# List of surplus blocks of a mixture-of-experts layer: with a slot per partition, by small products, in three steps

## The chip, the cores and the metric

The kernel runs on one core of a Trainium2 chip. The metric is the device time of one execution in microseconds (us); the time before is the median of three runs. The engines are TensorE (PE, with its weight loads shown apart as PEld), VectorE (DVE), ScalarE (ACT), GpSimd (POOL) and SyncE (SP), which issues the weight loads to the DMA engines.

## What is computed

One decoder layer on 1024 tokens of width 1024: a token mixer (a projection, two convolutional branches, gates, an output projection), a mixture of experts with 32 experts of which each token takes two, an embedding gate, and a final norm. What the change touches is the expert part. The reference sorts the 2048 assignments by expert, pads each expert's rows to blocks of 128 and runs every block:

```python
flat_e = expert_id.reshape(n_assign)              # 2048 assignments
counts = jnp.bincount(flat_e, length=N_EXPERTS)   # rows of each of 32 experts
padded = (counts + ROW_BLOCK - 1) // ROW_BLOCK * ROW_BLOCK
...
def expert_block(args):
    xb, e = args
    a = xb @ w_gate[e]
    b = xb @ w_up[e]
    return (jax.nn.silu(a) * b) @ w_down[e]
```

## The kernel before

The token mixer fills the first 830 us; w_o and the router follow, then the experts (950 to 1490 us), then the embedding gate and the final norm. All arithmetic is in fp32 or in products of split fp32 parts.

**Slots.** The 32 experts are put into 32 slots by rank of their row count. Each slot has a kind, a letter in SLOTS, that fixes how many rows it computes: L 32 rows, N 64, M 128, S 96, X 160, B 256 (two blocks of 128), A 352 in three units. Which expert sits in a slot is known on the chip only (slots, srow). Blocks of 128 rows are "wide" (class Wide): each weight tile is split into two parts on ACT and DVE (split, L99 and L100), in 24 parts a unit through a ring of four, and each part gives three products a block (L869). Narrower blocks (class Rows) multiply the unsplit weights (L928 gate and up, L955 down).

**The loop.** For unit u in order of slots: the activation of u (L932), the first three quarters of the first half of gate and up of u+1, the transposes of u's hidden rows into bank h and their copy (L941, L942), the last of that half, **a step of the list if the slot is in SIZES (18, 19, 21, 22)**, p_step (from slot 18 on it transposes p through banks x0 and x1, L110, and copies them out on DVE, L1164; later it multiplies them, L1173), the down product of u (L955), the copies of its result into ys (L966, half on ACT, half on DVE), and the transposes of unit u+2's gathered rows into x0 (and x1 for some), copied to its activation tile xt (L819 and L821; for wide blocks L828 and the splits). PE, ACT, DVE and SP issue in the order in which the program is written; POOL's order is a scheduler's.

**The list.** A slot may get more rows than its kind has. The surplus goes in blocks of 128 through a loop behind the last slot, guarded by the number of blocks. Its list (ovi: 30 experts, 30 first rows, one count) is worked out on DVE in one partition, in four steps: sizes0 (blocks of each slot by eight compares, a running sum by five shifts and adds), sizes1 and sizes2 (compares of 30 entries by 32 slots, 960 elements, and their sums), sizes3 (scaling and casts). The steps sizes1 and sizes2 take a scratch tile from the ring of three that holds the activation tiles: xtile(), mp.tile([128, 2048], dt, name="xt", bufs=3).

**Weights.** Six loads of 1 MB a slot, issued by SP (L678) into a pool of 1 MB buffers (about three slots' worth); a buffer comes free when the products of its slot are done, or for wide slots when its last part is split.

Of the kernel before, what the change touches and what calls it, by code (L numbers as in the profile page):

```python
# [10 lines left out]
F32 = mybir.dt.float32  # L11
# [5 lines left out]
OP = mybir.AluOpType  # L17
AX = mybir.AxisListType
# [5 lines left out]
NT = 8  # L24
KT = 8
KB = 31
NE = 32
DE = 512
CAP = 1024
# [3 lines left out]
NOV = 30  # L33
# [7 lines left out]
PARTS = 4  # L41

RETIRE = 42
SIZES = (18, 19, 21, 22)


A0, A1, A2, B1, B2, B3 = range(6)
# [20 lines left out]
def layer_kernel(ctx: ExitStack, tc: tile.TileContext, A, out, dbg=None):  # L68
    nc = tc.nc
    w_in = A["w_in"][0]  # L70
    dram = ctx.enter_context(tc.tile_pool(name="dram", bufs=1, space=DRAM))
    const = ctx.enter_context(tc.tile_pool(name="const", bufs=1))
# [11 lines left out]
    def tpsum():  # L84
        return psum.tile([128, 512], F32, name="tp", bufs=2)
# [27 lines left out]
    ident = const.tile([128, 128], F32, name="ident")  # L113
# [17 lines left out]
    place = const.tile([NE, NE], F32, name="place")  # L131
    cap_row = const.tile([1, NE], F32, name="cap_row")
    srow = const.tile([1, 2, NE], F32, name="srow")
    iota_s = const.tile([1, NE], F32, name="iota_s")
    ovi = const.tile([1, 2 * NOV + 1], I32, name="ovi")


# [38 lines left out]
    with tc.tile_pool(name="s0", bufs=1, side="right") as s0:  # L176
# [39 lines left out]
        with tc.manual_schedule(engines={mybir.EngineType.Pool, mybir.EngineType.DVE, mybir.EngineType.Activation}):  # L216
# [3 lines left out]
            tp = tpsum()  # L220
# [12 lines left out]
        tp = tpsum()  # L233
# [7 lines left out]
    with tc.tile_pool(name="s1", bufs=2) as s1:  # L241
        for cb in range(8):
# [18 lines left out]
            for t in (1, 2):  # L261
                nc.vector.scalar_tensor_tensor(c3, m[:, t:t + T], cw[:, cb, KB + t:KB + t + 1], c3,
                                               op0=OP.mult, op1=OP.add)
# [3 lines left out]
            for t in range(1, KB):  # L267
                nc.vector.scalar_tensor_tensor(acc, u[:, t:t + T], cw[:, cb, t:t + 1], acc,  # L268
                                               op0=OP.mult, op1=OP.add)
# [3 lines left out]
    rt = mix.enter_context(tc.tile_pool(name="rt", bufs=1, side="right"))  # L273
# [14 lines left out]
            nc.gpsimd.iota(pay[:, :, k, j], pattern=[[128, NT]], base=T * k * j, channel_multiplier=1)  # L288
    iota_e = rt.tile([128, NE], F32, name="iota_e")
    nc.gpsimd.iota(iota_e, pattern=[[1, NE]], base=0, channel_multiplier=0, allow_small_or_imprecise_dtypes=True)  # L290
    nc.gpsimd.tensor_copy(iota_s, iota_e[0:1])
    iota_r = rt.tile([128, 64], F32, name="iota_r")
    nc.gpsimd.iota(iota_r, pattern=[[1, 64]], base=0, channel_multiplier=0, allow_small_or_imprecise_dtypes=True)

# [25 lines left out]
        nc.gpsimd.memset(rank_row[:, s:s + 1], float(r))  # L320
    for s in range(NE):
        nc.gpsimd.memset(cap_row[:, s:s + 1], float(ROWS[s]))
    e_col = rt.tile([NE, 1], F32, name="e_col")
    nc.gpsimd.iota(e_col, pattern=[[0, 1]], base=0, channel_multiplier=1, allow_small_or_imprecise_dtypes=True)
    nc.gpsimd.memset(idx[64:, 5], OOB)
    acum = rt.tile([128, NE], BF16, name="acum")
# [454 lines left out]
    def bank(name):  # L781
        return banks.tile([128, 512], F32, name=name)


    mp = ctx.enter_context(tc.tile_pool(name="mp", bufs=1))

    def xtile(dt=F32):

        return mp.tile([128, 2048], dt, name="xt", bufs=3)
# [4 lines left out]
    ys = mp.tile([128, 2 * D], F32, name="ys")  # L794
    ix2 = mp.tile([128, 2], I32, name="ix2")
    novp = mp.tile([1, 1], I32, name="novp")
    ov_s = mp.tile([1, 4, NOV], F32, name="ov_s")
    nb = mp.tile([1, 1, NE], F32, name="nb")
    cums = [mp.tile([1, NE], F32, name=f"cum{i}") for i in range(2)]
    ysc, freeb, nxt = [], ["p0", "p1", "p2", "p3", "p4"], {"xg": 0, "y": 0, "hid": 0, "part": 0}  # L800

    def turn(what):
# [52 lines left out]
    class Wide:  # L855
# [15 lines left out]
        def gate_up(self, k, j, w):  # L871
            self.mm(self.b[j], [self.x[:, a, k] for a in range(2)], w, k == 0, k == KT - 1)
# [123 lines left out]
            return idx0[:r]  # L996
        return (idxf if e < FIXED else idx)[:r, b, e]

    cum_of = []

    def sizes(step):

        if step in (1, 2):
            s = xtile()[0:1]
            le, eq = (s[:, i * NOV * NE:(i + 1) * NOV * NE].rearrange("p (i s) -> p i s", i=NOV) for i in range(2))
        (sizes0, sizes1, sizes2, sizes3)[step](*((le, eq) if step in (1, 2) else ()))

    def sizes0():

        nc.vector.tensor_tensor(cums[0], srow[:, 0], cap_row, op=OP.subtract)  # L1010
        nc.vector.tensor_scalar(nb[:, 0], cums[0], 0.0, None, op0=OP.is_gt)
        for j in range(1, NT):
            nc.vector.scalar_tensor_tensor(nb[:, 0], cums[0], 128.0 * j, nb[:, 0], op0=OP.is_gt, op1=OP.add)
        cum, nxt = cums
        nc.vector.tensor_copy(cum, nb[:, 0])
        sft = 1
        while sft < NE:
            nc.vector.tensor_copy(nxt[:, :sft], cum[:, :sft])
            nc.vector.tensor_tensor(nxt[:, sft:], cum[:, sft:], cum[:, :NE - sft], op=OP.add)
            cum, nxt = nxt, cum  # L1020
            sft *= 2
        cum_of.append(cum)

    def sizes1(le, eq):
        cum = cum_of[0]

        nc.vector.tensor_tensor(le, cum[:, None, :].to_broadcast([1, NOV, NE]),
                                iota_s[:, :NOV, None].to_broadcast([1, NOV, NE]), op=OP.is_le)
        nc.vector.tensor_reduce(ov_s[:, 0], le, axis=AX.X, op=OP.add)
        nc.vector.tensor_tensor(le, le, nb.to_broadcast([1, NOV, NE]), op=OP.mult)  # L1030
        nc.vector.tensor_reduce(ov_s[:, 1], le, axis=AX.X, op=OP.add)
        nc.vector.tensor_tensor(ov_s[:, 2], iota_s[:, :NOV], ov_s[:, 1], op=OP.subtract)

    def sizes2(le, eq):

        nc.vector.tensor_tensor(eq, iota_s[:, None, :].to_broadcast([1, NOV, NE]),
                                ov_s[:, 0][:, :, None].to_broadcast([1, NOV, NE]), op=OP.is_equal)
        nc.vector.tensor_tensor(le, eq, srow[:, 1:2].to_broadcast([1, NOV, NE]), op=OP.mult)
        nc.vector.tensor_reduce(ov_s[:, 0], le, axis=AX.X, op=OP.add)
        nc.vector.tensor_tensor(le, eq, cap_row[:, None, :].to_broadcast([1, NOV, NE]), op=OP.mult)  # L1040
        nc.vector.tensor_reduce(ov_s[:, 1], le, axis=AX.X, op=OP.add)

    def sizes3():
        cum = cum_of[0]
        nc.vector.scalar_tensor_tensor(ov_s[:, 2], ov_s[:, 2], 128.0, ov_s[:, 1], op0=OP.mult, op1=OP.add)
        nc.vector.tensor_scalar(ov_s[:, 3], ov_s[:, 2], float(CAP - 128), None, op0=OP.min)
        nc.vector.tensor_copy(ovi[:, :NOV], ov_s[:, 0])
        nc.vector.tensor_copy(ovi[:, NOV:2 * NOV], ov_s[:, 3])
        nc.vector.tensor_copy(ovi[:, 2 * NOV:], cum[:, NE - 1:])

    blocks = {}

# [184 lines left out]
    for u, (e, _) in enumerate(UNITS):  # L1237
# [18 lines left out]
        for i, b in enumerate(blocks[u]):  # L1256
            b.hpose()
            if i == 0:
                gate_up(u + 1, (3,), 9)
        if first and e in SIZES:  # L1260
            sizes(SIZES.index(e))
        if u + 2 < len(UNITS) and UNITS[u + 1][0] != UNITS[u + 2][0]:
# [164 lines left out]
    for i, (a, b) in enumerate(cuts):  # L1427
        o = bank("h")[:, :256] if i == 2 else ps[i][:, :b - a]
        for k in range(KT):
            for j, w in PASSES:  # L1430
                nc.tensor.matmul(o, XW[tb % 2][:, j, k, :], GW[k // 2][w][:, k % 2, a:b],  # L1431
                                 start=(k == 0 and j == 0 and w == 0), stop=(k == KT - 1 and j == 1))
# [39 lines left out]
```

## Time and profile before

| | us |
|---|---|
| median of 3 runs (lowest, highest) | 1613.79 (1608.89, 1615.7) |
| the profiled execution | 1614.1 |
| its span, first to last instruction | 1612.4 |
| PE busy in the span | 1527.9 (95%) |
| PE weight loads busy | 1109.2 (69%) |
| DVE busy | 910.8 (56%) |
| ACT busy | 446.1 (28%) |
| POOL busy | 174.2 (11%) |

The profile page comes from one execution. Its shares are means over stages with different limits, so what a step is worth is read from the stage where it stands: which wait ends last there. A line of the code can be a helper's: all splits have lines 99 and 100, all weight loads line 678.

### The profile page before, as it was taken

The page shows a single profiled execution, that of the slowest core. Times are in us where ns is not written, and L with a number is a line of the kernel's source. Part 1 is how long each engine was busy: PE and PEld are TensorE (multiplying, and loading weights), DVE is VectorE, ACT ScalarE, POOL GpSimd, SP SyncE. Part 2 cuts the span into 40 slices and gives each one's busy share as a digit, 9 for nine tenths or more (in the row PEclk, how much of TensorE's full clock was granted, in tenths as well). Part 3 has the DMA queues.
Part 4 walks back from the last instruction along what each step waited for, and adds up shares of the span by engine and source line. Part 5 has one row for each costly group of instructions (what it writes and reads, how often), then busy time and mean ns, then how long its engine had stood idle before and what let it go on. Part 6 is the DMA issues. An engine that isn't in the chain of part 4 may idle for free. (4 is left out here: it accounts for less than half of the span.)

```text
span 1612.4 us, 21419 instructions
## 1 busy us (share of the span) xinstructions
PE 1527.9 (95%) x8328; PEld 1109.2 (69%) x8328; DVE 910.8 (56%) x1266; ACT 446.1 (28%) x695; POOL 174.2 (11%) x318
## 2 busy tenths in 40 slices
PE   6999999999999999999999959999999989988898
PEld 5888888888888888888877834346456555433686
DVE  5899999999983341534454432135454444421664
ACT  5212112212211221742231111024344322411443
POOL 3300000000000000000011222111111101110131
PEclk9999999999999999999999979999999999999899
DMA  5221121111126343434466589999999988999641
GB/s 174 64 66 59 46 66 62 57 53 58 61 66 209 95 154 91 157 118 143 144 231 214 183 315 377 404 408 405 403 409 383 335 325 328 405 406 406 256 170 52
DMA packets 190673, 336.80 MB, mean 209 GB/s; under 512 B 10182, under 2 KB 85022, under 8 KB 190560
## 3 DMA queue, kind: packets, MB, share of 16 engines
q1 hardware_dynamic: 173968, 284.10, 48.7%
q0 software_dynamic: 10576, 29.96, 5.1%
q10 hardware_dynamic: 6016, 21.27, 4.0%
q8 instruction: 67, 1.10, 0.3%
q14 instruction: 46, 0.38, 0.1%
HBM read 302.67 MB, written 35.11 MB: 209 GB/s over the span
## 5 line engine op out<-in xcount | busy, mean ns | idle before, releaser
L166 PE MATMUL mm<-a,wh 128*128 128x512 f32 x1792 | 554.6, 390 | 0.3 <-ACT a L211 0.3
L166 PEld LDWEIGHTS mm<-a,wh 128*128 128x128 f32 x1792 | 336.1, 188 | 70.2 <-ACT a L211 0.9
L166 PE MATMUL mm<-a,wl 128*128 128x512 f32 x896 | 349.2, 390 | 0.0
L268 DVE SCALAR_TENSOR_TENSOR acc<-u,cw,acc 128x1024 f32<-128x1024 f32 x240 | 307.9, 1283 | 7.9 <-ACT acc L251 1.9
L99 ACT ACTIVATE wh<-wraw 128x1024 fp32r<-128x1024 f32 x72 | 76.4, 1062 | 495.1 <-PE mm L166 423.1
L166 PEld LDWEIGHTS mm<-a,wl 128*128 128x128 f32 x896 | 168.4, 188 | 34.5
L869 PE MATMUL p<-d,xt 128*128 128x512 f32 x648 | 162.3, 403 | 3.4 <-DVE d L100 3.2
L166 PE MATMUL mm<-b,wh 128*128 128x512 f32 x512 | 157.7, 389 | 0.0
L869 PEld LDWEIGHTS p<-d,xt 128*128 128x128 f32 x648 | 120.1, 190 | 41.2 <-DVE d L100 6.4
L100 DVE TENSOR_TENSOR wl<-wraw,wh 128x1024 fp32r<-128x1024 f32 x72 | 87.8, 1219 | 73.2 <-ACT wh L99 73.1
L928 PE MATMUL p<-a,xt 128*32 128x256 f32 (+1 forms) x744 | 116.4, 455 | 2.5 <-DMA a<-in_w_exp_up_dram 1.9
L928 PE MATMUL p<-b,xt 128*32 128x256 f32 (+1 forms) x704 | 106.1, 444 | 4.6 <-DMA b<-in_w_exp_gate_dram 3.0
L166 PEld LDWEIGHTS mm<-b,wh 128*128 128x128 f32 x512 | 96.1, 188 | 20.0
L166 PE MATMUL mm<-b,wl 128*128 128x512 f32 x256 | 99.6, 389 | 0.0
L437 PE MATMUL mm<-b,a 128*128 128x512 f32 x384 | 96.0, 399 | 1.5 <-DVE b L100 1.3
L966 DVE COPY ys<-p 32x256 f32<-32x256 f32 (+1 forms) x51 | 25.0, 491 | 101.0 <-ACT ys L966 97.9
L437 PEld LDWEIGHTS mm<-b,a 128*128 128x128 f32 x384 | 69.5, 188 | 16.7 <-DVE b L100 2.3
L966 ACT COPY ys<-p 32x256 f32<-32x256 f32 (+1 forms) x51 | 21.3, 417 | 178.0 <-PE p L955 173.7
L928 PEld LDWEIGHTS p<-b,xt 128*32 128x32 f32 (+1 forms) x704 | 32.2, 116 | 49.4 <-issue 39.7
L928 PEld LDWEIGHTS p<-a,xt 128*32 128x32 f32 (+1 forms) x744 | 35.9, 118 | 42.6 <-issue 29.8
L100 DVE TENSOR_TENSOR d<-b,d 128x512 fp32r<-128x512 f32 x80 | 53.6, 688 | 18.2 <-ACT d L99 17.8
L99 ACT ACTIVATE d<-b 128x512 fp32r<-128x512 f32 x80 | 48.8, 628 | 27.1 <-PE p L869 13.8
(342 smaller groups left out, 1637.9 us busy)
## 6 DMA issues: line engine op xcount, KB each, us to landing
a<-in_w_exp_down_dram SPq DMA_DIRECT2D x35, 1024.0 KB
a<-in_w_exp_gate_dram SPq DMA_DIRECT2D x29, 1024.0 KB
wraw<-in_w_in_dram SPq DMA_DIRECT2D x56, 512.0 KB
a<-in_w_exp_up_dram SPq DMA_DIRECT2D x28, 1024.0 KB
b<-in_w_exp_gate_dram SPq DMA_DIRECT2D x28, 1024.0 KB
b<-in_w_exp_up_dram SPq DMA_DIRECT2D x27, 1024.0 KB
b<-in_w_exp_down_dram SPq DMA_DIRECT2D x26, 1024.0 KB
ut<-u_dram ACTq DMA_DIRECT2D x24, 512.0 KB
```

The source lines that it names most:

```text
L99: nc.scalar.activation(h, src, AF.Copy)
L100: nc.vector.tensor_tensor(l, src, h.bitcast(F32), op=OP.subtract)
L166: nc.tensor.matmul(ps[:, hf], w[wi][:, k], act[ai][k][:, hf * 512:(hf + 1) * 512], start=(k == 0 and i == 0), stop=(k == KT - 1 and i == 2))
L268: nc.vector.scalar_tensor_tensor(acc, u[:, t:t + T], cw[:, cb, t:t + 1], acc, op0=OP.mult, op1=OP.add)
L437: nc.tensor.matmul(ps[-1][:, hf], act(a, k), w(b, k)[:, hf * 512:(hf + 1) * 512], start=(k == 0 and i == 0), stop=(k == nk - 1 and i == 2))
L869: nc.tensor.matmul(o, x[a], w[b], start=first and i == 0, stop=last and i == 2)
L928: nc.tensor.matmul(self.gu[j][p:p + r], self.x[:, k], w[:, i:i + self.gu[0].shape[1]], start=(k == 0), stop=(k == KT - 1))
L966: (nc.scalar.copy if c < len(self.d) // 2 else nc.vector.tensor_copy)(self.y[:, c * n:(c + 1) * n], d)
```

## The change

The list is worked out with a slot in each of 32 partitions, in three steps at slots 13, 15 and 17. sizes0 turns the rows of counts, experts and capacities into columns by three transposes on PE and counts each slot's blocks by one compare of eight columns and one sum. sizes1 makes the running sum and the total by two products with a triangular matrix (upper), and from them a matrix with a one where an entry belongs to a slot (seq). sizes2 takes each entry's expert and first row by two products with that matrix, and writes ovi. The products go to bank x0. The scratch tile from the xt ring is gone; iota_s grows to 32 partitions, e_col moves to a pool that lives on.

```diff
-SIZES = (18, 19, 21, 22)
+SIZES = (13, 15, 17)
...
-    iota_s = const.tile([1, NE], F32, name="iota_s")
+    iota_s = const.tile([NE, NE], F32, name="iota_s")
+    e_col = const.tile([NE, 1], F32, name="e_col")
...
-    nc.gpsimd.tensor_copy(iota_s, iota_e[0:1])
+    nc.gpsimd.tensor_copy(iota_s, iota_e[:NE])
...
+    upper = mp.tile([NE, NE], F32, name="upper")
+    scol = mp.tile([NE, 8], F32, name="scol")
+    seq, sle = (mp.tile([NE, NE], F32, name=i) for i in ("seq", "sle"))
+    ov_s = mp.tile([1, NOV], F32, name="ov_s")
...
     def sizes(step):
-
-        if step in (1, 2):
-            s = xtile()[0:1]
-            le, eq = (s[:, i * NOV * NE:(i + 1) * NOV * NE].rearrange("p (i s) -> p i s", i=NOV) for i in range(2))
-        (sizes0, sizes1, sizes2, sizes3)[step](*((le, eq) if step in (1, 2) else ()))
+        (sizes0, sizes1, sizes2)[step]()
...
     def sizes0():
+        tp = bank("x0")
+        for i, row in enumerate((srow[:, 0], srow[:, 1], cap_row)):
+            nc.tensor.transpose(tp[:NE, i:i + 1], row, ident[:1, :1])
+        nc.vector.tensor_copy(scol[:, :3], tp[:NE, :3])
+
+        nc.vector.tensor_tensor(w_s, n_s, cap_s, op=OP.subtract)
+        nc.vector.tensor_scalar(sle[:, :NT], iota_s[:, :NT], 128.0, w_s, op0=OP.mult, op1=OP.is_lt)
+        nc.vector.tensor_reduce(nb_s, sle[:, :NT], axis=AX.X, op=OP.add)
+        nc.vector.tensor_scalar(upper, iota_s, e_col, None, op0=OP.is_ge)
+
+    def sizes1():
+        tp = bank("x0")
+        nc.tensor.matmul(tp[:NE, 0:1], upper, nb_s, start=True, stop=True)
+        nc.tensor.matmul(tp[0:1, 1:2], nb_s, upper[:, NE - 1:], start=True, stop=True)
+        nc.vector.tensor_copy(ovi[:, 2 * NOV:], tp[0:1, 1:2])
+        nc.vector.tensor_copy(to_s, tp[:NE, 0:1])
+        nc.vector.tensor_tensor(from_s, to_s, nb_s, op=OP.subtract)
+
+        nc.vector.tensor_scalar(sle, iota_s, to_s, None, op0=OP.is_ge)
+        nc.vector.scalar_tensor_tensor(seq, iota_s, from_s, sle, op0=OP.is_ge, op1=OP.subtract)
+        nc.vector.scalar_tensor_tensor(w_s, from_s, -128.0, cap_s, op0=OP.mult, op1=OP.add)
+
+    def sizes2():
+        tp = bank("x0")
+        nc.tensor.matmul(tp[0:1, :NOV], e_s, seq[:, :NOV], start=True, stop=True)
+        nc.tensor.matmul(tp[0:1, NE:NE + NOV], w_s, seq[:, :NOV], start=True, stop=True)
+        nc.vector.tensor_copy(ovi[:, :NOV], tp[0:1, :NOV])
+        nc.vector.scalar_tensor_tensor(ov_s, iota_s[0:1, :NOV], 128.0, tp[0:1, NE:NE + NOV], op0=OP.mult, op1=OP.add)
+        nc.vector.tensor_scalar(ovi[:, NOV:2 * NOV], ov_s, float(CAP - 128), None, op0=OP.min)
```

On DVE, in slot 19 before: behind the copy of the hidden rows (xt<-h) and two weight splits (d<-) stand the five operations of sizes1 (lines 1027 to 1032), then p_step's copies of x0 and x1 (L1164), then slot 19's ys copy and the activation tile of slot 21 (L821).

```order
L942 COPY xt<-h 128x256
L100 TENSOR_TENSOR d_7571<-b_6438,d_7570 128x512
L100 TENSOR_TENSOR d_7571<-a_5905,d_7570 128x512
L1027 TENSOR_TENSOR xt<-cum_6463,iota_s 1x960
L1029 TENSOR_REDUCE ov_s<-xt 1x30
L1030 TENSOR_TENSOR xt<-xt,nb 1x960
L1031 TENSOR_REDUCE ov_s<-xt 1x30
L1032 TENSOR_TENSOR ov_s<-iota_s,ov_s 1x30
L1164 COPY b_6467<-x_9636 128x512
L1164 COPY b_6467<-x_9642 128x512
L966 COPY ys<-p_9648 64x512
```

The same place on DVE in the changed kernel; its lines above 1000 are other numbers, and p_step's copies are L1151.

```order
L943 COPY xt<-h 128x256
L100 TENSOR_TENSOR d_7572<-b_6438,d_7571 128x512
L100 TENSOR_TENSOR d_7572<-a_5905,d_7571 128x512
L1151 COPY b_6468<-x_9635 128x512
L1151 COPY b_6468<-x_9641 128x512
L987 UNCONDITIONAL_BRANCH
L967 COPY ys<-p_9647 64x512
L822 COPY xt<-x_9670 128x512
```

The five operations are gone from between the splits and p_step's copies.

On PE, in slot 13 of the changed kernel: the last products of slot 14's gate and up for this point (p<-d), the three transposes of sizes0 into x0, the down product of slot 13 (L956) and the transposes of slot 15's rows into x0 (L820). Before, the rows are the same without the two of L1010.

```order
L870 MATMUL p_8415<-d_7572,xt 128x512
L870 MATMUL p_8415<-d_7571,xt 128x512
L1010 MATMUL x_8482<-ident,srow 32x1 x2
L1010 MATMUL x_8482<-ident,cap_row 32x1
L956 MATMUL p_8493<-b_6292,xt 32x256 x8
L956 MATMUL p_8493<-a_6181,xt 32x256 x8
L820 MATMUL x_8526<-ident,c_5282 128x32 x8
```

Three transposes now stand between slot 14's products and slot 13's down product.

On DVE at that place: behind slot 13's copy of the hidden rows and two splits of slot 14 come the five operations of sizes0, ahead of the ys copy.

```order
L943 COPY xt<-h 128x128
L100 TENSOR_TENSOR d_7572<-b_6255,d_7571 128x512
L100 TENSOR_TENSOR d_7572<-b_6466,d_7571 128x512
L1011 COPY scol<-x_8482 32x3
L1013 TENSOR_TENSOR scol<-scol 32x1
L1014 TENSOR_SCALAR sle<-iota_s,scol 32x8
L1015 TENSOR_REDUCE scol<-sle 32x1
L1016 TENSOR_SCALAR upper<-iota_s,e_col 32x32
L967 COPY ys<-p_8493 32x256 x2
```

Before, the ys copy followed the two splits. On POOL, the iota of e_col moves from the router's constants to the front of the program, and the memset of idx from there to behind the first operation of the first row norm.

## Rows read from the trace of the kernel before

**Rows 1.** The page: busy time, share of the span and instructions of PE and of its weight loads, and the span in 40 slices (busy tenths of PE; of the DMA engines).

```profile
PE 1527.9 (95%) x8328; PEld 1109.2 (69%) x8328; DVE 910.8 (56%) x1266; ACT 446.1 (28%) x695; POOL 174.2 (11%) x318
...
PE   6999999999999999999999959999999989988898
...
DMA  5221121111126343434466589999999988999641
```

**Rows 2.** Stretches of the span: from and to, length, busy time of PE, PEld, DVE, ACT and POOL with counts, granted clock of PE, DMA share, GB/s.

```profile
1220.00:1303.60 83.60, 79.48 (x558) 52.30 (x546) 39.49 (x83) 28.83 (x53) 10.14 (x11) 1.00 0.98 362
1303.60:1360.00 56.40, 50.35 (x272) 30.94 (x276) 30.80 (x42) 15.31 (x26) 6.78 (x7) 0.94 0.79 292
1360.00:1480.00 120.00, 110.09 (x846) 50.87 (x840) 38.89 (x76) 28.13 (x54) 13.17 (x15) 0.96 1.04 406
...
1300.00:1310.00 10.00, 4.36 (x24) 1.80 (x24) 6.19 (x8) 2.15 (x4) 0.00 (x0) 0.90 1.04 414
1310.00:1320.00 10.00, 10.00 (x36) 8.01 (x36) 5.72 (x9) 3.00 (x5) 2.19 (x2) 0.76 0.74 263
1340.00:1360.00 20.00, 19.99 (x151) 9.69 (x153) 10.16 (x13) 2.93 (x5) 4.59 (x5) 1.00 0.81 303
```

**Rows 3.** What PE waited for from 1160 to 1370 us, longest first: us in total, times, longest. The first, the second and the last of six groups; the three between also name DVE.

```profile
PE x L819 <- issue: 5.6, 1, 5.6
PE x L828 <- DVE xt L100: 2.3, 2, 1.2
...
PE x L828 <- DVE b L1164: 0.5, 1, 0.5
```

**Rows 4.** Instructions in order of time in slots 19 and 20: start, length, engine, line, operation, count, idle time before and what ended it.

```profile
1298.98 1.03 PE L110 MATMUL x<-ident,b 128*128 128x128 f32 x8
1299.94 1.94 PE L955 MATMUL p<-b,xt 128*64 128x512 f32 x8
...
1301.71 1.89 PE L955 MATMUL p<-c,xt 128*64 128x512 f32 x8
...
1303.65 1.15 DVE L1027 TENSOR_TENSOR xt<-cum,iota_s 1x960 f32<-1x960 f32 x1 [5.82 <-PE p L955]
...
1308.46 1.27 DVE L1164 COPY b<-x 128x512 f32<-128x512 f32 x2
1309.24 1.08 PE L819 MATMUL x<-ident,xg 64*128 64x64 f32 x8 [5.64 <-issue]
...
1310.25 13.32 PE L869 MATMUL p<-d,xt 128*128 128x512 f32 x48
1310.49 0.69 DVE L821 COPY xt<-x 128x512 f32<-128x512 f32 x1
...
1323.50 2.80 PE L928 MATMUL p<-b,xt 128*64 128x512 f32 x12
```

**Rows 5.** The same view in slots 8 and 9, which have the same two kinds.

```profile
1088.61 1.94 PE L955 MATMUL p<-b,xt 128*64 128x512 f32 x8
...
1092.80 11.51 PE L869 MATMUL p<-d,xt 128*128 128x512 f32 x48
...
1093.64 0.42 DVE L821 COPY xt<-x 128x256 f32<-128x256 f32 x1
...
1104.24 1.50 PE L928 MATMUL p<-a,xt 128*32 128x256 f32 x24
```

**Rows 6.** The same view in slot 18, around sizes0 of before.

```profile
1276.08 0.17 DVE L1010 TENSOR_TENSOR cum<-srow,cap_row 1x32 f32<-1x32 f32 x1
...
1280.13 0.74 ACT L966 COPY ys<-p 32x256 f32<-32x256 f32 x2 [6.95 <-PE p L955]
1280.20 1.25 PE L828 MATMUL x<-ident,c 128*128 128x128 f32 x8 [0.47 <-DVE b L1164]
...
1280.89 1.20 ACT L99 ACTIVATE xt<-x 128x512 fp32r<-128x512 f32 x2
...
1282.56 1.25 PE L828 MATMUL x<-ident,c 128*128 128x128 f32 x8 [1.10 <-DVE xt L100]
```

**Rows 7.** The same view at the head of the expert stage: the nearest small operations.

```profile
944.25 0.27 DVE L641 TENSOR_SCALAR place<-rank_row,col 32x32 f32<-32x32 f32 x1
...
944.58 0.26 PE L646 MATMUL tp<-place,col 32*1 32x32 f32 x2 [2.39 <-DVE place L641]
944.66 0.29 PE L647 MATMUL tp<-place,e_col 32*1 32x32 f32 x2
...
945.12 0.20 DVE L649 COPY srow<-tp 1x64 f32<-1x64 f32 x1
```

**Rows 8.** The same view at the places where the new steps stand: slot 13, and the last row slot 17.

```profile
1178.71 1.07 PE L955 MATMUL p<-b,xt 128*32 128x256 f32 x16
...
1180.57 0.68 PE L819 MATMUL x<-ident,c 32*128 32x32 f32 x8
...
1181.47 0.85 DVE L966 COPY ys<-p 32x256 f32<-32x256 f32 x2 [2.89 <-ACT ys L966]
...
1268.28 0.59 PEld L955 LDWEIGHTS p<-b,xt 128*32 128x32 f32 x16 [0.30 <-DVE xt L942]
```

**Rows 9.** The same view at the start, POOL alone.

```profile
2.14 0.15 POOL L325 MEMSET idx<- 64x64 int32 x1
```

**Rows 10.** What PE waited for from 1360 to 1520 us: the longest wait that a DMA ended.

```profile
PE p L928 <- DMA b<-in_w_exp_gate_dram: 3.0, 1, 3.0
```

More of the change, by code (lines that the diff above doesn't have):

```diff
@@ L322, in layer_kernel @@
         nc.gpsimd.memset(cap_row[:, s:s + 1], float(ROWS[s]))
-    e_col = rt.tile([NE, 1], F32, name="e_col")
     nc.gpsimd.iota(e_col, pattern=[[0, 1]], base=0, channel_multiplier=1, allow_small_or_imprecise_dtypes=True)
@@ L796, in layer_kernel @@
     novp = mp.tile([1, 1], I32, name="novp")
-    ov_s = mp.tile([1, 4, NOV], F32, name="ov_s")
-    nb = mp.tile([1, 1, NE], F32, name="nb")
-    cums = [mp.tile([1, NE], F32, name=f"cum{i}") for i in range(2)]
+    upper = mp.tile([NE, NE], F32, name="upper")
+    scol = mp.tile([NE, 8], F32, name="scol")
+    seq, sle = (mp.tile([NE, NE], F32, name=i) for i in ("seq", "sle"))
+    ov_s = mp.tile([1, NOV], F32, name="ov_s")
     ysc, freeb, nxt = [], ["p0", "p1", "p2", "p3", "p4"], {"xg": 0, "y": 0, "hid": 0, "part": 0}
@@ L997, in places @@
         return (idxf if e < FIXED else idx)[:r, b, e]
-    cum_of = []
+    n_s, e_s, cap_s, nb_s, to_s, from_s, w_s = (scol[:, i:i + 1] for i in range(7))
     def sizes(step):
-        if step in (1, 2):
-            s = xtile()[0:1]
-            le, eq = (s[:, i * NOV * NE:(i + 1) * NOV * NE].rearrange("p (i s) -> p i s", i=NOV) for i in range(2))
-        (sizes0, sizes1, sizes2, sizes3)[step](*((le, eq) if step in (1, 2) else ()))
+        (sizes0, sizes1, sizes2)[step]()
     def sizes0():
[L1010 to L1049, printed above, removed]
+        tp = bank("x0")
+        for i, row in enumerate((srow[:, 0], srow[:, 1], cap_row)):
+            nc.tensor.transpose(tp[:NE, i:i + 1], row, ident[:1, :1])
```

## Prediction

> **What bounds the kernel now.** I read the page first, then stretches of the span, then PE's waits, and last the order of time around each step that the change touches. The page [rows 1] shows PE busy nearly everywhere and the DMA engines full from about slice 22 on, with a dip around slices 31 to 34: the expert stage is held by the weight stream for most of its length, but not there. The stretches say the same in numbers [rows 2]: up to 1303.6 us the DMA share is 0.98, from 1303.6 to 1360 only 0.79, from 1360 on 1.04, which is its ceiling here. So in the dip the weight buffers are full and loads wait for PE to give buffers back. PE's waits from 1160 to 1370 [rows 3] are six groups, and none ends on a DMA. In the dip the chain is PE, and a microsecond lost by PE is lost by the loads behind it. One wait is far above the rest: 5.6 us, a single time, in front of line 819, with no releaser named.
>
> **That wait, followed by hand.** In order of time [rows 4]: PE transposes part of p into banks x0 and x1 (L110, 1298.98), runs the down product of slot 19 (1299.94 to about 1303.6), and next wants x0 again for the transposes of slot 21 (L819). x0 is free once DVE has copied it out (L1164). But on DVE that copy stands behind the second step of the list, and its first operation (L1027) writes a scratch tile that takes the place of slot 19's activations, so it starts only when the down product has read them: at 1303.65, after DVE stood idle. The step then keeps DVE until 1308.46, the first copy of x0 takes some 0.6 us, and L819 starts at 1309.24. The wait is thus 4.8 us of step, 0.6 of copy and 0.2 of signalling: the copy's end and PE's start fit, which is my reason to name the releaser that the view leaves out. The granted clock is 0.90 in 1300 to 1310, where PE stood, and 0.76 in the ten us after [rows 2]; the 48 products behind the wait take from 1310.25 to 1323.50.
>
> **The change, part by part.** I sum against the profiled execution, 1614.1 us (span 1612.4 and 1.7 around it); the median of the runs shown, 1613.8, is 0.3 below it.
>
> (1) The second step leaves slot 19, and with it the scratch tile. What would be left there can be read: slots 8 and 9 are the same two kinds, N and then B, with no step between [rows 5]. From the start of the down product to the first product of the slot after next, slots 8 and 9 take 1104.24 - 1088.61 = 15.63 us, slots 19 and 20 take 1323.50 - 1299.94 = 23.56 us. The difference, 7.93 us, holds the wait and what the lower clock cost behind it. One thing differs: the next slot's activations are copied 128x512 at slot 21 and 128x256 at slot 10 (0.69 against 0.42 us, L821), and this copy stands before the first weight split on DVE. That can keep 0.3, and at the far end one whole weight part of the eight (11.51 us / 8 = 1.4). I take 7.6 gained, bounds 6.5 and 7.9.
>
> (2) The first step leaves slot 18. It held DVE from 1276.08 to about 1279.5, and PE started L828 0.47 us late behind L1164 [rows 6]. But bank x0 is next split by ACT at 1280.89, straight after its copy of ys (1280.13, 0.74), which waits for the down product alone; and the second L828 (1282.56) waits for the splits. With the 0.47 gone, ACT is next late, at the same time. I take 0; the far end is 0.5 gained.
>
> (3) The old third and fourth steps leave slots 21 and 22. PE is busy 19.99 of 20 us in 1340 to 1360 [rows 2], where the third one stood on DVE. Nothing waited: 0.
>
> (4) Seven small products come onto PE, in slots 13, 15 and 17, where PE is the chain too. The nearest rows are the two products of 1 by 32 in L646 and L647 [rows 7]: four instructions between 944.58 and 944.95, so at most 0.19 us a product and 1.3 for seven. The lower end is 0.07 each (eight L819 transposes of 32 columns fit in 0.68 us [rows 8], less the first one's latency), 0.5 together. In slot 17 PE's weight load already waits 0.30 us for DVE at this point [rows 8], which hides two of them. I take 0.6 lost, bounds 0.2 to 1.3. None of them waits for data: the inputs of a step are ready two slots before.
>
> (5) Fourteen small DVE operations take the place of 35. The nearest rows are 0.17 to 0.27 us each [rows 6, 7] (L641, with a column as operand, is the dear end), so five, six and three of them take about 1.1, 1.2 and 0.6 us. What hides them is the down product after each: in slot 13 it runs from 1178.71 and the next use of x0 starts at 1180.57, 1.9 us later, while DVE's next work, the ys copy, starts at 1181.47 [rows 8]. x0 needs only the first operation of step one (the first two of the others). If that cover were gone, each place would cost up to 1.2 us.
> The Trainium skill, page VectorE: DVE Perf Modes, section on the TRN2 errata, speaks against this part: each instruction that reads SBUF pays a fixed latency, so it advises tiles of at least 512 elements, and the change goes from 960 elements to 32 or fewer. By its measured fixed term of about 150 cycles fourteen operations come to an estimated 2.4 us, by the rows to 2.9; the fixed part is paid 14 times in place of 35, so the rule weighs on the single operation and not on the sum.
>
> (6) On POOL an iota moves to the front and the memset of idx (0.15 us [rows 9]) behind the first step of the first row norm. DVE and PE wait there for POOL: 0.1 lost, at most 0.2. The copy of iota_s is off the path.
>
> **Sum at slot 21:** 7.6 - 0.6 - 0.1 = 6.9 us earlier.
>
> **Does it reach the end?** What is next late is the weight stream. DMA in 1303.6 to 1360 is idle for 56.4 x (1 - 0.79/1.04) = 13.6 us [rows 2]; taking 6.9 from that leaves 6.7, so the loads can follow PE. From 1360 on the stream runs full, with PE waiting for it only here and there (3.0 us the longest [rows 10]); it fills earlier by what PE is earlier and ends earlier by as much. I take the whole 6.9: 1614.1 - 6.9 = 1607.2, and 0.3 less against the median: **1607**, or -0.42%.
>
> **Rivals.**
> *B, the stream takes it back.* The weight stream is the true limit and the dip only shows it waiting in another form. For it: the share of 1.04 before and after. Against it: 13.6 us of idle in the dip, and no PE wait on a DMA there. If half to nearly all is given back: 1610 to 1613.5.
> The Trainium skill, Trainium Kernel Development and Optimization, section Performance Expectations, says that matmul busy time tells badly how close a kernel is to its limit, and weight-load busy time tells it better; here that is 69% against 95% [rows 1]. By that rule PE has room and case B gains weight; the row of the dip speaks against it.
> *C, the stall moves to slot 13; slower than before.* Slot 13 is narrow and is followed by a wide one, as slot 19 is, and its first DVE operation stands behind two weight splits. If it ends later than 1180.57, the transposes into x0 wait for DVE as they did at 1309, and the clock falls as it did: up to the 7.9 us measured there, paid while 7.6 are gained, plus 0.6 and 0.1 and up to 1.2 at each of two places: 1614.1 + 1.0 to 3.4, or 1615 to 1617.5. Against it: it needs DVE to be 1.9 us behind the products, and the splits before it are done with the products of slot 14.
> *D, the change doesn't remove the wait.* If the 5.6 us belong to something else at L819 (a branch on PE, the gather that fills xg), they stay, and the small products come on top: 1614.1 + 0.2 to 1.5, about 1615. Against it: L819 starts 0.15 us after the copy of x0 ends.
>
> **How the numbers follow.** Forecast 0.70, B 0.14, C 0.07, D 0.09. Runs of this kernel spread over 7 us, so about 0.5% (8 us, below 1605.7 or above 1621.9) is what a measurement can tell from no change. The forecast lies 1.3 us on the near side of that bound. Its own range: 7.9 gained at (1), 0.5 at (2) and 0.2 lost at (4) gives 1605.6; 6.5 gained and 1.3 and 0.2 lost gives 1608.8; with the spread of a median, about 2.5 either way, 1603 to 1611.5. So some 0.30 of its 0.70 is faster by over 0.5%, and 0.40 within. B and nearly all of C and D are within. Faster 0.31, same 0.64, slower 0.05. For the range I go up to 1613, which takes in most of B, and leave C and D out; below I go to 1601.5, for a clock that also holds better in later slots than I count.
>
> **What would show it.** Right: no wait over 1 us in front of the transposes behind slot 19's down product; the copies L1164 right behind their transposes, under the down product; the granted clock near 1.00 where it was 0.76; from the down product of slot 19 to the first product of slot 21 near 16 us; slot 21 earlier by about 7 us and the last load by as much. Steps (4) and (5): the new products within 0.4 us a place, and the x0 transposes of slots 15, 17 and 19 with no wait on DVE. Wrong, case B: slot 21 starts 7 us earlier but PE waits for DMA in slots 22 to 30 grow by some us. Case C: a wait on DVE in slot 13 behind the down product. Case D: the wait before slot 21 is still there.

## The result

The changed kernel is slower. Its median is 1622.85 us of nine runs (1619.67 to 1625.98), that of the kernel before beside it 1614.94 us of nine (1608.89 to 1616.09); the ratio is 1.0061, with an interval of 1.0048 to 1.0073. The forecast was 1607, in a range of 1601.5 to 1613. Of the runs below, one of e1 and one of the kernel before beside e9 took 1945 and 1946 us at a granted clock of 0.75 where the others have 0.98, and the medians and ratios given here leave these two out.

The wait that the prediction followed is gone. In order of time, the changed kernel around the down product of slot 19 (start, length, engine, line, operation, count, idle time before; L956, L1151, L820, L870, L822 and L929 are L955, L1164, L819, L869, L821 and L928 of [rows 4]):

```profile
1311.12 1.29 DVE L1151 COPY b<-x 128x512 f32<-128x512 f32 x2 [1.77 <-PE x L110]
1311.45 1.94 PE L956 MATMUL p<-b,xt 128*64 128x512 f32 x8
...
1315.03 0.71 PE L820 MATMUL x<-ident,xg 64*128 64x64 f32 x8
1315.67 1.88 PE L870 MATMUL p<-d,xt 128*128 128x512 f32 x7
...
1327.35 2.80 PE L929 MATMUL p<-b,xt 128*64 128x512 f32 x12
```

The copies of x0 and x1 now lie under the down product, the transposes L820 follow it with no wait, and from the down product to the first product of slot 21 it takes 1327.35 - 1311.45 = 15.90 us where it took 23.56 [rows 4]: 7.66 us gained. But everything stands later: the down product of slot 19 starts at 1311.45 and not at 1299.94. What PE waited for from 1160 to 1370 us, longest first, has no 5.6 us any more, and it has a DMA, which [rows 3] did not have:

```profile
PE x L829 <- DVE xt L100: 3.0, 2, 1.8
...
PE p L929 <- DMA b<-in_w_exp_up_dram: 1.4, 1, 1.4
...
PE p L870 <- issue: 0.4, 1, 0.4
```

The stretches say why. First one of the kernel before that [rows 2] do not hold, then three of the changed kernel (columns as in [rows 2]):

```profile
1000.00:1200.00 200.00, 189.96 (x1278) 98.75 (x1280) 84.69 (x144) 65.81 (x120) 31.84 (x32) 0.99 1.04 405
```

```profile
1000.00:1200.00 200.00, 187.41 (x1226) 95.63 (x1227) 82.08 (x144) 64.61 (x117) 29.64 (x30) 0.98 1.04 386
...
1303.60:1360.00 56.40, 55.71 (x273) 34.02 (x273) 21.71 (x34) 16.33 (x28) 5.01 (x5) 1.00 0.96 348
1360.00:1480.00 120.00, 108.16 (x808) 50.18 (x804) 36.92 (x67) 27.78 (x53) 13.89 (x15) 0.93 1.04 387
```

The DMA share is 1.04 in both kernels, but the bytes fell: 405 to 386 GB/s from 1000 to 1200 us, where the changed kernel's first step of the list does not come before 1184, and 406 to 387 behind the list's steps [rows 2]. The DMA engines are as full as before and move 4.7% less. In the dip the share is 0.96 where it was 0.79, so little is left there of the idle time that was to carry PE's gain. That alone does not show the loss: in e2 below the share of this stretch is 0.98, and the gain comes through.

The starts of the activations (L932, L933; in slot 20, which is wide, L875, L876) give the account by slot, each from one profiled execution. They are counted here from the product that places the experts (L646), which starts at 944.58 us before, 944.51 after, 945.51, 945.30 and 943.15 in the three experiments of the table:

| us from L646 to the activation of | before | after | e1: before, buffers 32 bytes on | e2: after, buffers back | e7: before, other scratch |
|---|---|---|---|---|---|
| slot 8 | 132.41 | 139.48 | 137.80 | 134.62 | 134.31 |
| slot 16 | 265.03 | 274.72 | 274.10 | 269.69 | 268.54 |
| slot 19 | 342.89 | 354.48 | 350.38 | 346.33 | 346.35 |
| slot 20 | 378.21 | 382.13 | 385.47 | 374.01 | 373.99 |
| slot 31 | 541.78 | 552.13 | 555.47 | 537.21 | 537.10 |

Two of these rows (slot 31 before, then after):

```profile
1486.36 0.38 ACT L932 ACTIVATE hid<-p 64x256 f32<-64x256 f32 x1 [0.97 <-PE p L928]
```

```profile
1496.64 0.38 ACT L933 ACTIVATE hid<-p 64x256 f32<-64x256 f32 x1 [0.97 <-PE p L929]
```

After is 7.1 us late by slot 8, before any step of the list runs, and 11.6 by slot 19; there 7.7 come back, and by slot 31 it is 10.4 late again. Single executions of one expert part scatter by some us in this count (see "What stays open" below).

### The profile page after: what moved, and what is told of

Its sections match the earlier page's. It is cut to its first block, busy times and chain, and to the rows that moved or that the text cites. A ratio compares the mean times of both kernels' runs of the same rounds, so it can differ in the third digit from the quotient of the medians.

```text
span 1624.2 us, 21421 instructions
## 1 busy us (share of the span) xinstructions
PE 1538.4 (95%) x8339; PEld 1110.3 (68%) x8339; DVE 899.4 (55%) x1245; ACT 446.7 (28%) x695; POOL 174.4 (11%) x318
## 5 line engine op out<-in xcount | busy, mean ns | idle before, releaser
L870 PE MATMUL p<-d,xt 128*128 128x512 f32 x648 | 160.9, 400 | 4.4 <-DVE d L100 3.7
L870 PEld LDWEIGHTS p<-d,xt 128*128 128x128 f32 x648 | 118.3, 188 | 42.6 <-DVE d L100 7.3
L929 PE MATMUL p<-a,xt 128*32 128x256 f32 (+1 forms) x744 | 121.4, 466 | 7.0 <-DMA a<-in_w_exp_gate_dram 3.6
L929 PE MATMUL p<-b,xt 128*32 128x256 f32 (+1 forms) x704 | 110.2, 447 | 6.8 <-DMA b<-in_w_exp_up_dram 6.2
L929 PEld LDWEIGHTS p<-a,xt 128*32 128x32 f32 (+1 forms) x744 | 37.1, 121 | 53.3 <-issue 37.4
L929 PEld LDWEIGHTS p<-b,xt 128*32 128x32 f32 (+1 forms) x704 | 32.6, 117 | 52.1 <-issue 35.2
```

What stands on the lines that cost most here:

```text
L870: nc.tensor.matmul(o, x[a], w[b], start=first and i == 0, stop=last and i == 2)
L929: nc.tensor.matmul(self.gu[j][p:p + r], self.x[:, k], w[:, i:i + self.gu[0].shape[1]], start=(k == 0), stop=(k == KT - 1))
```

## The experiments

**Theory A, the address.** The pool const lies ahead of the weight buffers. It ends in a tile named pad of 104 words, which in the kernel before puts the first buffer at byte 20480 of a partition, a multiple of 512. The changed kernel puts one more tile into const, e_col, which takes 32 bytes, so all buffers that weights land in (a, b, c, d) start 32 bytes past such a multiple, and nearly every tile that is allocated behind them moves by 32 bytes too. Theory A: that start costs the stream its rate. The rival for e1 and e2 is that the steps themselves, or their new places, cost the time. W, L and S in the later expectations are about the scratch tile of sizes1: whether the wait for it or the length of the step cost the time in slot 19, and whether the old steps would stall at other slots too.

**e1: the kernel before, all buffers 32 bytes on.**

```diff
-    const.tile([128, 104], F32, name="pad")
+    const.tile([128, 112], F32, name="pad")
```

> The kernel before with nothing changed but the pad ahead of the weight buffers, 32 bytes longer, so that the buffers start at 20512 in each partition, where the changed kernel has them, and not at 20480. Theory A (start address): the added column e_col moved every weight buffer by 32 bytes, and the DMA engines write there more slowly; then this kernel shows 385 to 390 GB/s in 1050 to 1100 us and in the last full stretch (406 before), with the DMA share still 1.04, and takes 1626 to 1634 us. Theory R (the rate belongs to the execution or to the place of the inputs in HBM, and the new steps themselves cost the 8 us): 400 to 408 GB/s and 1613 to 1617 us.

1626.14 us (three runs) against 1613.89: 1.0084, interval 1.0055 to 1.0112. Its stretches:

```profile
1000.00:1200.00 200.00, 187.39 (x1224) 95.34 (x1225) 82.12 (x141) 65.31 (x118) 30.06 (x30) 0.97 1.04 387
...
1360.00:1480.00 120.00, 105.89 (x769) 49.17 (x769) 41.17 (x76) 27.61 (x52) 13.86 (x15) 0.94 1.04 387
```

Not one operation differs from before, only where the tiles lie, and the rate is that of after. A holds, and its rival falls.

**e2: the changed kernel, buffers back at 20480.**

```diff
-    const.tile([128, 104], F32, name="pad")
+    const.tile([128, 96], F32, name="pad")
```

> The changed kernel with the pad 32 bytes shorter, so that the weight buffers start at 20480 again; all else as changed. Theory A: 405 GB/s, no wait over 1 us before slot 21's transposes, and the prediction's sum comes back: 1605 to 1610 us, 5 to 9 below the kernel before. Theory R: as the changed kernel, 1620 to 1626 us.

1605.81 us (six runs) against 1613.89: 0.9955, interval 0.9938 to 0.9973; its span is 1605.7. Its stretches:

```profile
1000.00:1200.00 200.00, 188.13 (x1229) 96.23 (x1230) 82.61 (x144) 65.64 (x118) 29.11 (x29) 0.97 1.04 404
...
1360.00:1480.00 120.00, 109.29 (x847) 50.89 (x849) 38.15 (x70) 28.35 (x54) 12.86 (x14) 0.97 1.04 408
```

The rate is back, and the rest of the change is worth 0.45%, about what the prediction said of the whole (0.42%).

**e3, e8, e4: the kernel before, buffers 64, 128 and 256 bytes lower.** The pad has 88, 72 and 40 words, so the buffers start at a multiple of 64, of 128 and of 256 and of no higher power.

> The kernel before with the pad 64 bytes shorter: the weight buffers start at 20416, a multiple of 64 and not of 128. If 64 bytes are enough: 405 GB/s and 1612 to 1617 us. If it takes 128 or more: 385 to 390 GB/s and 1626 to 1634 us. Theory R: 1612 to 1617 us.

> The kernel before with the pad 128 bytes shorter: the weight buffers start at 20352, a multiple of 128 and not of 256. If 128 bytes are enough: 405 GB/s and 1611 to 1617 us. If it takes 256: 387 to 391 GB/s and 1624 to 1630 us, as at 32 and 64 bytes.

> The kernel before with the pad 256 bytes shorter: the weight buffers start at 20224, a multiple of 256 and not of 512. If 256 bytes or less are enough: 405 GB/s and 1612 to 1617 us. If it takes 512: 385 to 390 GB/s, 1626 to 1634 us.

64: 1627.56 us, 1.0095 (1.0072 to 1.0118). 128: 1625.18 against 1612.18, 1.0076 (1.0054 to 1.0098). 256: 1612.95, 0.9999 (0.9981 to 1.0017). From 1360 to 1480 us, in this order:

```profile
1360.00:1480.00 120.00, 105.86 (x776) 49.08 (x779) 40.39 (x75) 27.62 (x52) 13.86 (x15) 0.94 1.04 388
```

```profile
1360.00:1480.00 120.00, 107.90 (x774) 49.34 (x776) 40.93 (x75) 27.60 (x52) 13.85 (x15) 0.91 1.04 389
```

```profile
1360.00:1480.00 120.00, 107.22 (x838) 50.40 (x832) 38.47 (x75) 27.76 (x53) 12.87 (x14) 0.99 1.04 407
```

Of the starts tried, a multiple of 256 is enough, and 32, 64 and 128 cost the same within the intervals.

**e5: the changed kernel, buffers at 20480, its steps at the old places.**

```diff
-SIZES = (13, 15, 17)
+SIZES = (18, 19, 21)
...
-    const.tile([128, 104], F32, name="pad")
+    const.tile([128, 96], F32, name="pad")
```

> The changed kernel's steps at slots 18, 19 and 21 in place of 13, 15 and 17, weight buffers at 20480. Theory S (what cost 7.6 us was the length of the step on DVE and its wait for the scratch tile, not the slot): the 5.6 us in front of slot 21's transposes stay away; p's transposes into x0 wait for DVE's first operations of the step, some 0.5 us at each of slots 18 and 19: 1605 to 1610 us. Theory P (the slot: any step between the splits and p's copies in slot 19 stops PE there): 1611 to 1616 us, with a wait of several us in front of slot 21's transposes.

1605.83 us (12 runs) against 1612.18: 0.9961 (0.995 to 0.9973), as e2: S holds, P falls. In slots 18 and 19 the transposes of p into x0 now follow the small products in the same bank, and wait little:

```profile
1277.76 1.09 PE L110 MATMUL x<-ident,b 128*128 128x128 f32 x8 [0.24 <-DVE scol L1011]
...
1300.62 1.09 PE L110 MATMUL x<-ident,b 128*128 128x128 f32 x8 [0.30 <-DVE scol L1023]
```

So to the short steps the new slots are worth nothing; that they are short and have no scratch tile is worth it all (e7 parts these two).

**e6: the kernel before with the new slots.**

```diff
-SIZES = (18, 19, 21, 22)
+SIZES = (13, 15, 17, 18)
```

> The kernel before with its four old steps at slots 13, 15, 17 and 18 in place of 18, 19, 21 and 22, buffers at 20480. Theory S: the wait at slot 19 is gone, but the steps with a scratch tile still wait for a down product and keep DVE 5 to 6 us at slots 15 and 17, where slot 18's hidden rows come next on DVE: a wait of 1 to 4 us on PE there: 1607 to 1612 us. Theory P: 1604 to 1608 us, as the changed kernel with aligned buffers.

1609.95 us (12 runs) against 1612.18: 0.9987 (0.9974 to 1.0001), not to be told from no change. The 5.6 us are gone, and another wait of PE has come (same stretch as [rows 3]):

```profile
PE p L928 <- issue: 3.0, 1, 3.0
```

It stands in slot 17, with the third step on DVE ahead of it (the first and the last of its 960-element operations, the copy into the next activation tile, PE's products of that tile):

```profile
1268.00 1.14 DVE L1036 TENSOR_TENSOR xt<-iota_s,ov_s 1x960 f32<-1x960 f32 x1
...
1272.71 1.14 DVE L1041 TENSOR_REDUCE ov_s<-xt 1x30 f32<-1x960 f32 x1
...
1274.77 0.69 DVE L821 COPY xt<-x 128x512 f32<-128x512 f32 x1
...
1275.56 4.44 PE L928 MATMUL p<-b,xt 128*64 128x512 f32 x12 [2.98 <-issue]
```

So old steps do stall PE at the new slots, as S said, 3.0 us in place of 5.6, and the median gains 2.2 us where e5, beside the same runs of before, gains 6.4. But here DVE had no idle time ahead of the step, so it did not wait for its scratch: it is the step's 5.9 us (1268.00 to 1273.85), with the ys copy behind it, that hold back L821. That PE's products waited for L821 is read from the times alone, as they start 0.1 us behind that copy; the releaser is again not named.

**e7: the kernel before, only the scratch of sizes1 moved**, from the xt ring to the half of ys that the next slot will write. The step keeps its place, its five operations and their length; the ring hands out one tile less.

```diff
         if step in (1, 2):
+            if step == 1:
+                i = nxt["y"] % 2
+                s = ys[0:1, i * D:i * D + 960]
+                sizes1(s.rearrange("p (i s) -> p i s", i=NOV), None)
+                return
             s = xtile()[0:1]
```

> The kernel before with one thing changed: the second step, at slot 19, takes its scratch from the half of ys that slot 19 writes next, and not from the ring of activation tiles. Its five operations keep DVE as long as before, 4.8 us. Theory W (the wait for the scratch tile puts the step behind the down product): the step runs from about 1297.8 to 1302.6 under the down product, p's copies follow, slot 21's transposes wait under 0.5 us: 1605 to 1609 us. Theory L (the length alone): they still wait 3 us or more: 1610 to 1615 us.

1603.12 us (six runs) against 1612.18: 0.9944 (0.9928 to 0.9961), the lowest median here, though the interval overlaps those of e2 and e5. The profiled execution is the slowest of the six (1607.98). Slot 19 in order of time, with the step's first operation, its last, p's copies and the transposes:

```profile
1299.78 1.14 DVE L1032 TENSOR_TENSOR ys<-cum,iota_s 1x960 f32<-1x960 f32 x1
...
1304.49 0.18 DVE L1037 TENSOR_TENSOR ov_s<-iota_s,ov_s 1x30 f32<-1x30 f32 x1
1304.59 1.27 DVE L1169 COPY b<-x 128x512 f32<-128x512 f32 x2
1305.54 0.70 PE L819 MATMUL x<-ident,xg 64*128 64x64 f32 x8
```

The step still takes 4.9 us (1299.78 to 1304.67), but it starts ahead of p's transposes and not behind the reads of the down product (1303.65 in [rows 4]), and p's first copy ends under that product, so that L819 follows it with no wait. In slot 19 it was the wait for the scratch tile, not the length of the step: W holds and L falls there (in slot 17 of e6 the length counted).

**e9: the kernel before, only b, c and d 32 bytes on, a in place.**

```diff
     bufA = [big.tile([128, 2048], F32R, name=f"a{i}") for i in range(8)]
+    big.tile([128, 8], F32, name="padb")
     bufB = [big.tile([128, 2048], F32R, name=f"b{i}") for i in range(8)]
```

> The kernel before with 32 bytes put in between the eight buffers a and the eight buffers b, so that a start at 20480 and every 8192 bytes on, and b, c and d 32 bytes past a multiple of 256. Some 92 of 193 loads go to a. Theory A per buffer: the aligned loads move at 406 GB/s and the others at 387, so 394 to 399 GB/s in 1050 to 1100 us and in 1360 to 1480, and 1616 to 1623 us. Theory all-or-none (one shifted buffer slows the whole stream): 385 to 390 GB/s, 1624 to 1630 us.

1637.74 us (four runs) against 1611.68: 1.0154 (1.0131 to 1.0177). The expected time, 1616 to 1623, is missed. The experts are not the reason: from L646 to the activation of slot 31 it takes 548.19 us, 6.4 more than before, where e1 takes 13.7 more; half the buffers cost about half, as A says by buffer. Every tile behind b moved as in e1, so the 7.3 us between the two belong to the buffers a, which take about half of the loads, and little is left for the tiles that no weights land in. From 1000 to 1200 us the rate lies between the two, and from 1018.4 to 1218.4, the same stretch counted from L646, it is 395 GB/s:

```profile
1000.00:1200.00 200.00, 188.74 (x1351) 95.20 (x1352) 74.27 (x132) 57.32 (x107) 31.74 (x32) 0.98 1.04 392
```

But L646 itself starts at 962.96, 18.4 us late. The token mixer is slower: its products from 60 to 940 us, grouped by operands (busy time, mean ns of one), of before and then of e9:

```profile
L166 PE MATMUL mm<-a,wh 128*128 128x512 f32 x1692 | 521.4, 389 | 0.0
L166 PE MATMUL mm<-a,wl 128*128 128x512 f32 x846 | 329.2, 389 | 0.0
L166 PE MATMUL mm<-b,wh 128*128 128x512 f32 x512 | 157.7, 389 | 0.0
```

```profile
L167 PE MATMUL mm<-a,wh 128*128 128x512 f32 x1696 | 533.8, 396 | 0.0
L167 PE MATMUL mm<-a,wl 128*128 128x512 f32 x848 | 335.5, 396 | 0.0
L167 PE MATMUL mm<-b,wh 128*128 128x512 f32 x512 | 157.8, 389 | 0.0
```

The products of a, which stayed, with the split weights wh and wl, which moved, take 7 ns more, 18.7 us in sum; those of b, which moved with the weights, take what they took. In e1 all moved together, and the means are 390 and 389. Theory M: a product is slower when its two operands start at different offsets; rival N: the loads or splits into moved tiles are.

**e10, e11: the kernel before, wh and wl moved by 32 and by 64 bytes, the buffers a, b, c and d in place.** The mixer's working tiles behind wl (pools s1 and s2, read and written by ACT, DVE, POOL and DMA) move with them, which the expectation does not say; in e9 they moved too, and the products of b kept their 389 ns.

```diff
-    wring.tile([128, 184], F32, name="padw", bufs=1)
+    wring.tile([128, 192], F32, name="padw", bufs=1)
```

(e11 has 200.)

> The kernel before, with 32 bytes more per partition in front of the mixer's split weights wh and wl alone; the weight buffers a, b, c, d stay where they were. Theory M, on the part that the run with half of the buffers moved left open: a product of the mixer takes about 7 ns longer when its moving operand (a, b) and its weights (wh, wl) start at different offsets. In that run the products of a with wh and wl (2538 between 60 and 940 us) had 396 ns where they had 389, 18.7 us in sum, and those of b, which had moved with wh, stayed at 389. Here a and b both differ from wh: 3306 products by 7.4 ns, 24 us, so 1635 to 1640 us, means of 396 ns for both, and the rate of the stream after 1000 us unchanged at 405 to 408 GB/s. Rival N: the time there went to the loads into moved tiles or to the splits that write them; then nothing but the split tiles moves here, the means stay at 389 and the time at 1610 to 1616.

> The same with 64 bytes. If any difference of the two starts counts, or a difference within 256 bytes as for the transfers, 1635 to 1640 us with means of 396 ns. If only a difference within 64 bytes counts, the means stay at 389 and the time at 1610 to 1616. Rival N: 1610 to 1616.

1635.29 us, 1.0134 (1.0064 to 1.0204), and 1634.35 us, 1.0128 (1.0057 to 1.02), two runs each, against 1614.75 (three runs). In both, both kinds are slow now (e10, then one row of e11):

```profile
L166 PE MATMUL mm<-a,wh 128*128 128x512 f32 x1695 | 533.4, 396 | 0.0
...
L166 PE MATMUL mm<-b,wh 128*128 128x512 f32 x512 | 161.0, 396 | 0.0
```

```profile
L166 PE MATMUL mm<-a,wh 128*128 128x512 f32 x1693 | 531.8, 394 | 0.0
```

L646 starts at 968.20 and 966.50, 23.6 and 21.9 us late, where M said 24; the stream from 1050 to 1100 us has 409 GB/s in both. M holds, N falls, and e9's miss is M's 18.4 us on top of half of A. By slot 31 (from L646) the kernels with the old steps stand at 541.78, 542.07, 543.94 and 538.96 us with all weight buffers at a multiple of 256 (before, e4, e10, e11), at 555.47, 554.08 and 556.15 with none (e1, e3, e8), and at 548.19 with half (e9).

## Why the prediction was wrong

**The step that failed** is the sum: it has no term for e_col. That the tile moves to a pool that lives on stands in the text on the change, and the line of the pad stands a few lines below it in the kernel, but the list from (1) to (6) prices operations and waits only. The paragraph on whether the gain reaches the end then took the stream's rate from 1360 us on as given (406 GB/s), and no rival let it fall. The missing term, between after and e2, is 1622.85 - 1605.81 = 17.0 us in the medians, 14.9 in the table's last row; it turns the 8.1 us that e2 gains (1613.89 - 1605.81) into a loss.

**(1)** 7.6 was right: 7.66 in after, and 7.64 in e2 (1320.03 - 1304.11 = 15.92 us):

```profile
1304.11 1.94 PE L956 MATMUL p<-b,xt 128*64 128x512 f32 x8
...
1320.03 2.79 PE L929 MATMUL p<-b,xt 128*64 128x512 f32 x12
```

The releaser that the view does not name was p's copy behind the step, as the prediction read it: in e7 nothing but the scratch moves, the step and with it the copy come earlier, and the wait is gone.

**(2) and (3)** 0 and 0: the activations of slots 18 and 19 stand 14.66 us apart in before, which has the first step there, and in e2, which has not; 16.14 in after without it and 16.16 in e7 with it, so what makes the 1.5 us is not the step. The 0.47 us in front of the first L828 is gone in e2, and the wait for the splits in front of the second one is 1.80 where it was 1.10: what was next late was late, as the prediction said. Of slots 21 and 22, e7 still has the third and the fourth step and e2 none: from the activation of 21 to that of 22 it is 12.17 and 12.18 us, from there to that of 23 10.12 in both.

**(4)** 0.6 was right: in e2 the small products delay what follows by 0.15 us in slot 13, 0.20 in slot 15 and 0.19 in slot 17, 0.54 in all. The first two places:

```profile
1182.08 0.20 PE L1010 MATMUL x<-ident,srow 1*32 1x1 f32 x2
...
1182.23 1.07 PE L956 MATMUL p<-b,xt 128*32 128x256 f32 x16
...
1184.10 0.68 PE L820 MATMUL x<-ident,c 32*128 32x32 f32 x8
```

```profile
1208.62 0.22 PE L1020 MATMUL x<-scol,upper 32*32 32x1 f32 x2
...
1208.82 1.93 PE L956 MATMUL p<-a,xt 128*32 128x256 f32 x32
```

**(5)** Hidden, as said: L820 has no wait on DVE behind the down product. The fourteen operations take 0.14 to 0.24 us each, 2.43 in sum; the rows had made it 2.9. The estimate of 2.4 from the page VectorE: DVE Perf Modes of the Trainium skill, section on the TRN2 errata, was the nearer one.

**(6)** 0.1 is below what can be seen: L646 starts 0.07 us earlier in after, and in e2, e5, e6 and e7 anywhere from 943.15 to 945.97.

**The rivals.** C fell, there is no stall in slot 13. D fell with the wait. B's words fit after (slot 20 only 3.9 us late, slot 31 10.4 late, PE waiting for DMA), but its mechanism does not: it has the stream at its old rate, and at that rate (e2) the gain reaches the end: 8.1 us in the medians, and in the profiled execution 4.2 at slot 20 and 4.6 at slot 31. So what spoke against B, idle time of the stream in the dip, was rightly read.

**What stays open** is scatter: e2, e6 and e7, at the old rate, are 3 to 4 us behind the profiled execution of before by slot 19, e5 is not (342.48). Kernels whose expert part is that of before scatter as much there: e4 stands at 343.53, e10 at 345.81 and e11 at 339.84. So a difference of less than some 6 us between two single executions says little; that the starts are the cause rests on the medians, the rates and the groups by slot 31. No wait was found that explains the scatter.

## What to carry to other kernels

A tile added to or taken from a pool can move all that is allocated behind it: list the start of every DMA target and of every pair of operands of the hot products before and after, and price a moved start like a moved instruction. Put new small tiles behind the large ones, or give the pad's bytes for them, as e2 does. A scratch tile from a ring that other work uses brings that work's wait along; e7 gets the whole gain by taking a scratch that is free.

## What the runs showed of the hardware that was not expected

Weight loads into buffers that start 32, 128 or 192 bytes past a multiple of 256 in a partition (after and e1, e8, e3) run at 386 to 389 GB/s in the stretches from 1000 to 1200 and from 1360 to 1480 us, where loads at a multiple of 256 run at 402 to 408 (before, e2, e4 to e7), and the busy share of the DMA engines reads 1.04 either way: only the bytes tell. On this kernel that is 12 to 14 us (e1, e3, e8), and 17 between after and e2.

The Trainium skill, DMA: Bandwidth & Descriptors, section "How a descriptor splits into AXI transactions", says that a transfer which does not start at a 256-byte boundary begins its first transaction at the boundary below, so that the bytes in front are fetched for nothing. The runs agree on the 256 bytes (407 GB/s in e4 against 389 in e8). They show a loss where the start on the written side moves, and that section speaks of reading; whether its mechanism is the one at work here was not tested.

Products of 128x512 whose moving operand and weights differ by 32 or 64 bytes in where they start past a multiple of 256 take 394 to 396 ns by the view's mean where they take 389, at a granted clock of 1.00 in both: 18 to 24 us in this mixer (e9, e10, e11). Equal starts of 32 past it cost nothing that is seen (389 ns for b with wh in e9; 390 and 389 in e1). What makes it, and which other distances are free, wasn't tried.
